# Attention scores from halves of the array's rows instead of the whole array

## The chip, the cores and the metric

The kernel runs on one core of one Trainium2 chip. The metric is the device time of one execution in microseconds (us); the lower the better. The engines are TensorE (PE, with its loads of the stationary operand as PEld), VectorE (DVE), ScalarE (ACT), GpSimd (POOL) and SyncE (SP), which here only issues transfers (DMAs).

## The reference, cut to what matters

Two layers, each with three branches that read the same normalised input. The change lies in branch A, sliding-window attention over 1024 tokens with 16 query heads of 64 channels; 4 query heads share a group of keys and values.

```
s = jnp.einsum('bnqkgd,bnskd->bnkgqs', q, kk).astype(jnp.float32) * (A_HEAD_DIM ** -0.5)
...
s = s - slopes[:, :, None, None] * dist.astype(jnp.float32)
s = jnp.where(valid[None, :, None, None], s, -jnp.inf)
...
m = jnp.maximum(jnp.max(s, axis=-1, keepdims=True), sink)
p = jnp.exp(s - m)
probs = (p / (jnp.sum(p, axis=-1, keepdims=True) + jnp.exp(sink - m))).astype(vv.dtype)
o = jnp.einsum('bnkgqs,bnskd->bnqkgd', probs, vv)
```

Each block of 128 queries sees the 128 keys of its own block and the 128 before it. Branch B is gated linear attention, branch C an S5 scan; a projection in front and one behind hold most of the products.

## The kernel before

Everything is float32. A product that has to be exact is made of float32r products, which PE takes in one pass where a float32 product takes two passes: an operand is split into hi (rounded to float32r, by ACT) and lo (the rest, by DVE), and hi x hi, hi x lo and lo x hi are added up. `split` (L50) does it for weights, inputs and the like. Projections (`proj_T`, L387 to L389) give 24 such products of 128 x 512 for each half of the tokens.

In attention the channels of a head fill only 64 of the array's 128 rows. The kernel uses the other 64 for lo: `proj_aq` evicts a projection of two heads into `qs`, per head hi on partitions 0 to 63 and lo on 64 to 127, with two instructions each on ACT (L473) and DVE (L474), 64 partitions a piece. `keys` writes hi and lo of a group's keys into `kd`, each on both halves of the partitions, with two copies on ACT (L452) and two subtractions on DVE (L453). `attn_block` then needs two products of 128 rows per head (L588, L589): stationary [q hi; q lo], streamed [k hi; k hi] and [k lo; k lo], 256 columns each. So a block of 128 queries and two heads costs four products. Both heads' scores lie in one PSUM room, `sc`, taken from 6 common rooms (a bank each); projections have 2 of their own.

Behind the scores come, for each head, bias and maximum (DVE, L594), exponential (ACT, L599) and division (DVE, L601, L603), four transposes of the probabilities into `pT` (PE, L609), a split into `ph` and `pl` (ACT L52, DVE L53), the products with the values (PE, L619, L620) and the sum of their halves (ACT L622, DVE L626). Blocks overlap: `attention` emits for each of 8 pairs of heads and 8 blocks the first stage of a block, then pieces of the S5 scan (`s5_step`), of modulation sums (L135, L145) and of queued projections (`pump`), then the next stages of the blocks in flight. So 64 blocks a layer, 128 in all, are spread over the two attention stages. `keys` and `values` of the next group are called behind the last block of a group (first half of the tokens) and behind the second block of the next (second half).

A scheduler puts each engine's instructions in order; PE, DVE and ACT then run theirs strictly in that order, and SP its transfers.

Of the kernel before, what the change touches and what calls it, by code (L numbers as in the profile page):

```python
# [24 lines left out]
P = 128  # L25
# [10 lines left out]
# parts of M at the end of a layer: heads of branch A in pairs, branch B, branch C  # L36
# [5 lines left out]
class Trunk:  # L42
# [7 lines left out]
    def split(self, hi, lo, src):  # L50
        """hi = src rounded to float32r, lo = src - hi (exact in float32r)."""
        self.nc.scalar.copy(hi, src)  # L52
        self.nc.vector.tensor_tensor(out=lo, in0=src, in1=hi.bitcast(F32), op=ALU.subtract)  # L53
# [31 lines left out]
    def queue(self, name, gen, units=4):  # L85
        """units of products in a generator whose first step is to load; units = 0: no such step."""
        self.q.append([name, gen, units, units > 0])

    def prefetch(self, n=0):
        """emit the loads of the queue's entry n ahead of its products."""  # L90
        if len(self.q) > n and self.q[n][3]:
            next(self.q[n][1])
            self.q[n][3] = False

    def unit(self):
        """emit one unit of the queue; False if it is empty."""
# [18 lines left out]
    def finish(self, name=None):  # L115
        """emit the queue up to the end of the named entry, or all of it."""
# [7 lines left out]
    def rstd(self, ss, n, w=1):  # L124
        """(ss / n + EPS) ** -0.5 on a small tile, in place."""
# [12 lines left out]
    def mod_part(self, l, j):  # L138
        """512 columns at a time; j: shift 0, 1, scale 2, 3, gate * g_post 4, 5."""
# [42 lines left out]
    # ---- first layer's input: norm, transpose, modulation, split, by blocks of 256 columns; a_v grows with them  # L182
    def startup(self):
# [5 lines left out]
        # c, b_mod and g_pre with D on partitions  # L189
# [12 lines left out]
        def load(n):  # L202
            """256 rows of 512 columns for shift or scale."""
# [12 lines left out]
        # silu(c) = c * (1 + tanh(c / 2)) / 2  # L216
# [6 lines left out]
        # sums that grow side by side in a bank are one group, opened by a product with zeros  # L223
# [22 lines left out]
        # rows of w_mod whose products run on the tensor engine; the others are summed first  # L246
        direct = (((2, 5), (1, 2, 5)), ((2,), (5,)))

        def mods(b):
            """shift and scale of a half of the columns."""  # L250
# [27 lines left out]
        def prep(b, h):  # L278
            """half of the columns, half of the tokens."""
# [78 lines left out]
    def wsplit(self, shape, srcs):  # L358
        """load weights in chunks of 512 to 544 columns a partition and split them."""
# [15 lines left out]
    def proj_T(self, l, c0, sink):  # L375
        """Columns c0..c0+128 of h @ w_in, transposed: [128, tokens] in two halves."""
# [18 lines left out]
    def proj_tok(self, l, cols, sink):  # L395
        """Columns of h @ w_in, tokens on partitions; cols: list of (first, number)."""
# [38 lines left out]
    def proj_av(self, l):  # L435
        """a_v with tokens on partitions."""
# [3 lines left out]
    def proj_ak(self, l, pair):  # L440
        """keys of two groups, kept in float32."""
# [3 lines left out]
    def keys(self, g, half):  # L445
        """keys of a group in two parts, each on both halves of the partitions, half of the tokens."""
        nc = self.nc
        sl = slice(half * 512, (half + 1) * 512)
        src = self.M[64 * (g % 2):64 * (g % 2) + 64, 12 + g // 2, sl]
        for e in range(2):  # L450
            ps_ = slice(64 * e, 64 * e + 64)
            nc.scalar.copy(self.kd[ps_, 0, sl], src)  # L452
            nc.vector.tensor_tensor(out=self.kd[ps_, 1, sl], in0=src, in1=self.kd[ps_, 0, sl].bitcast(F32),  # L453
                                    op=ALU.subtract)

    def values(self, g, half):
        """values of a group in two parts, half of the tokens."""
# [6 lines left out]
    def proj_aq(self, l, pair):  # L464
        """queries of two heads, scaled, in two parts on the two halves of the partitions."""
# [3 lines left out]
        def sink(pj, half, ts_):  # L469
            q = qs[half]  # L470
            for h in range(2):
                src = pj[64 * h:64 * h + 64, :]
                nc.scalar.mul(q[0:64, h, :], src, 0.125)  # L473
                nc.vector.scalar_tensor_tensor(out=q[64:128, h, :], in0=src, scalar=0.125,  # L474
                                               in1=q[0:64, h, :].bitcast(F32),
                                               op0=ALU.mult, op1=ALU.subtract)
        return self.proj_T(l, OFF_AQ + pair * P, sink)

    def advance(self, flight, gen=None):
        """entries in flight: each advances by a stage as a new one enters."""  # L480
# [6 lines left out]
    def attention(self, l, side):  # L487
        """all pairs of heads; the S5 scans, the GLU and projections run between the blocks."""
# [30 lines left out]
        for pair in range(8):  # L519
# [10 lines left out]
            for b in range(NT):  # L530
# [24 lines left out]
                if pr == 1 and b == NT - 1 and g < 3:  # L555
                    self.finish(f"k{(g + 1) // 2}")
                    self.keys(g + 1, 0)
                    self.values(g + 1, 0)
# [3 lines left out]
        while flight:  # L562
# [3 lines left out]
            for _ in range(2):  # L566
                # the last two units gate what the last blocks put out
# [6 lines left out]
    def attn_block(self, pair, b, qs, bias):  # L574
        """128 queries of two heads; softmax over the scores of two blocks of keys and the sink."""
# [8 lines left out]
        sc = self.psum("sc")  # L584
        for h in range(2):
            lhs = qs[:, h, (b % 4) * P:(b % 4 + 1) * P]
            dst = sc[:, h * 256:(h + 1) * 256]
# [1014 lines left out]
```

## Time and profile before

| | |
|---|---|
| time, median of 3 runs | 1860.26 us (1858.48 to 1860.90) |
| span of the profiled execution | 1860.8 us, within the range of the runs |
| PE busy | 1749.4 us, 94% |
| DVE busy | 1353.2 us, 73% |
| ACT busy | 859.7 us, 46% |
| attention stages | about 360 to 780 us and 1240 to 1660 us |

PE's products are pipelined: a row's time runs to the modelled end of the product, which overlaps the next one, so the distance between two starts says what a product costs PE. A projection product of 512 streamed columns starts 0.23 us after the one before it. In the chain of work that ended last each piece is followed back to what released it. A float32 product has two rows for its two passes, a float32r product one.

### The profile page before, as it was taken

How to read it: one execution, taken by the hardware profiler on the slowest of the kernel's cores; microseconds unless marked ns; L12 is line 12 of the kernel's file. 1: busy time of each engine (PE TensorE's matmuls, PEld its weight loads, DVE VectorE, ACT ScalarE, POOL GpSimd, SP SyncE). 2: the span in 40 equal slices, each digit the busy share in tenths (PEclk: the TensorE clock that was granted, in tenths of full speed). 3: DMA queues.
4: the chain of work that ended last, by engine and by line, in shares of the span. 5: the costliest groups of instructions: out<-in, count | busy, mean ns of one | idle time of the engine just before them, and what ended most of it. 6: DMA issues, size and time to landing. Idle time of an engine off the chain costs nothing.

```text
span 1860.8 us, 28251 instructions
## 1 busy us (share of the span) xinstructions
PE 1749.4 (94%) x9403; PEld 1458.5 (78%) x9403; DVE 1353.2 (73%) x2975; ACT 859.7 (46%) x1973; POOL 589.0 (32%) x1005
## 2 busy tenths in 40 slices
PE   7999799999989989999998999999999899999998
PEld 5987688887777677788778878888878767878876
DVE  6986796579999798647676765954898978873534
ACT  5233333445556565446663242423555656642433
POOL 4279750212343454002217850401323511000100
PEclk7999999999999999999998999999999999999999
DMA  8143402235542322335464432222345111113342
GB/s 308 31 108 125 131 29 74 65 113 171 170 142 69 114 74 76 101 125 184 169 199 95 137 102 57 57 60 65 104 128 150 52 46 41 35 51 134 105 165 101
DMA packets 239385, 198.24 MB, mean 107 GB/s; under 512 B 49596, under 2 KB 195068, under 8 KB 239240
## 3 DMA queue, kind: packets, MB, share of 16 engines
q1 hardware_dynamic: 211640, 172.54, 30.9%
q10 hardware_dynamic: 25536, 16.80, 2.9%
q0 software_dynamic: 2064, 7.11, 1.0%
q8 instruction: 74, 1.21, 0.3%
q14 instruction: 71, 0.58, 0.1%
HBM read 163.13 MB, written 37.46 MB: 108 GB/s over the span
## 4 chain that ended last, share of the span: by engine, by line
PE 61%; DVE 21%; ACT 5%; issue 5%; POOL 4%; DMA 4%; SPq 0%; ACTq 0%; DVEq 0%; POOLq 0%
PE py L1472 14%; PE pj L387 9%; PE pj L389 9%; PE pj L388 9%; DVE wlo L53 2%; PE pj L1472 2%; PE pa L884 2%; PE pj L1370 2%; DVE p L594 2%; DVE pl L53 1%; PE pT L609 1%; PE pj L408 1%; PE pj L410 1%; PE pj L409 1%; DVE p L603 1%
## 5 line engine op out<-in xcount | busy, mean ns | idle before, releaser
L387 PE MATMUL pj<-H,whi 128*128 128x512 f32 x1088 | 442.8, 407 | 10.6 <-DVE M L1386 6.4
L389 PE MATMUL pj<-H,wlo 128*128 128x512 f32 x1088 | 431.7, 397 | 5.5 <-DVE wlo L53 5.5
L388 PE MATMUL pj<-H,whi 128*128 128x512 f32 x1088 | 431.0, 396 | 0.0
L53 DVE TENSOR_TENSOR wlo<-wraw,whi 128x512 fp32r<-128x512 f32 (+1 forms) x320 | 238.6, 765 | 87.2 <-ACT whi L52 86.5
L52 ACT CAST whi<-wraw 128x512 fp32r<-128x512 f32 (+1 forms) x320 | 191.4, 618 | 185.3 <-PE pj L388 108.9
L387 PEld LDWEIGHTS pj<-H,whi 128*128 128x128 f32 x1088 | 207.6, 191 | 56.4 <-DVE M L1386 7.2
L389 PEld LDWEIGHTS pj<-H,wlo 128*128 128x128 f32 x1088 | 207.1, 190 | 54.3 <-DVE wlo L53 7.4
L388 PEld LDWEIGHTS pj<-H,whi 128*128 128x128 f32 x1088 | 207.6, 191 | 40.9 <-issue 1.3
L599 ACT ACTIVATE p<-p,st 128x257 f32<-128x257 f32 (+1 forms) x256 | 125.7, 492 | 153.4 <-DVE st L594 133.4
L53 DVE TENSOR_TENSOR mlo<-M,mhi 128x384 fp32r<-128x384 f32 (+2 forms) x80 | 53.4, 675 | 141.8 <-ACT mhi L52 135.7
L1472 PE MATMUL py<-whi,mhi 128*128 128x512 f32 x448 | 142.4, 397 | 6.6 <-ACT whi L52 3.5
L1472 PE MATMUL py<-wlo,mhi 128*128 128x512 f32 x448 | 144.8, 396 | 0.6 <-DVE wlo L53 0.5
L1472 PE MATMUL py<-whi,mlo 128*128 128x512 f32 x448 | 143.3, 394 | 0.7 <-DVE mlo L53 0.7
L1493 POOL TENSOR_SCALAR yrs<-yss 128x1 f32<-128x1 f32 x16 | 6.7, 418 | 376.5 <-ACT junk L1489 375.4
L52 ACT CAST mhi<-M 128x384 fp32r<-128x384 f32 (+2 forms) x80 | 50.3, 634 | 158.4 <-PE pj L1472 92.7
L594 DVE CUSTOM_DVE_ANT_0 p<-sc,bias,sink 128x256 f32<-128x256 f32 (+1 forms) x256 | 111.4, 463 | 9.2 <-PE sc L589 8.1
L583 POOL COPY p<-sink 128x2 f32<-128x2 f32 x128 | 36.0, 283 | 220.9 <-PE pT L609 102.2
L1472 PEld LDWEIGHTS py<-whi,mhi 128*128 128x128 f32 x448 | 83.1, 188 | 28.9 <-ACT whi L52 6.7
L1472 PEld LDWEIGHTS py<-wlo,mhi 128*128 128x128 f32 x448 | 84.2, 188 | 22.9 <-DVE wlo L53 4.1
L1472 PEld LDWEIGHTS py<-whi,mlo 128*128 128x128 f32 x448 | 84.1, 188 | 20.0 <-DVE mlo L53 1.5
L410 PE MATMUL pj<-wlo,H 128*128 128x256 f32 (+1 forms) x320 | 92.9, 292 | 6.3 <-DVE wlo L53 6.3
L408 PE MATMUL pj<-whi,H 128*128 128x256 f32 (+1 forms) x320 | 93.6, 293 | 3.7 <-DVE hv L346 2.7
(380 smaller groups left out, 3931.8 us busy)
## 6 DMA issues: line engine op xcount, KB each, us to landing
wraw<-in_w_in_dram SPq DMA_DIRECT2D x160, 256.0 KB
wraw<-in_w_out_dram SPq DMA_DIRECT2D x160, 256.0 KB
wraw<-in_w_mod_dram SPq DMA_DIRECT2D x64, 256.0 KB
M<-s5tab SPq DMA_DIRECT2D x32, 256.0 KB
M<-s5turn SPq DMA_DIRECT2D x64, 128.0 KB
M<-in_w_mod_dram SPq DMA_DIRECT2D x10, 512.0 KB
s5tab<-O ACTq DMA_DIRECT2D x8, 512.0 KB
s5tab<-G ACTq DMA_DIRECT2D x8, 512.0 KB
```

The costliest lines, as they stand in the source:

```text
L52: self.nc.scalar.copy(hi, src)
L53: self.nc.vector.tensor_tensor(out=lo, in0=src, in1=hi.bitcast(F32), op=ALU.subtract)
L387: nc.tensor.matmul(pj, hi, hh, start=(k == 0), stop=False)
L388: nc.tensor.matmul(pj, hi, hl, start=False, stop=False)
L389: nc.tensor.matmul(pj, lo, hh, start=False, stop=(k == KD - 1))
L408: nc.tensor.matmul(pj[:, :N], hh, hi, start=(k == 0), stop=False)
L410: nc.tensor.matmul(pj[:, :N], hh, lo, start=False, stop=(k == KD - 1))
L594: nc.vector.tensor_tensor_reduce(out=p[:, h, 0:n], in0=sc[:, h * 256:h * 256 + n], in1=bias[:, h, o0:o0 + n], scale=-1.0, scalar=self.sink ...
L599: nc.scalar.activation(p[:, h, 0:n + 1], p[:, h, 0:n + 1], AF.Exp, bias=neg[:, h:h + 1], scale=-1.0, accum_out=den[:, h:h + 1])
L884: nc.tensor.matmul(pa[:, j * P:(j + 1) * P], X[:, c * P:(c + 1) * P], xq[:, :, c * 64:(c + 1) * 64], start=True, stop=True)
L1370: nc.tensor.matmul(pz, wg[:, k, :], self.M[:, MIX_C[k], ts_], start=(k == 0), stop=(k == 3))
L1472: self.nc.tensor.matmul(py[t, h], lhs, ws[h][w][:, 0, :], start=(n == 0 and first), stop=(n == N - 1 and last))
```

## The change

`keys` splits a group's keys once, on the half of the partitions on which they lie, and one DMA per half of the tokens (256 KB, on the SP queue) copies hi and lo to the other half. It is called for the first half of the next group's tokens behind the sixth block of the group's second pair, where it was behind the eighth; `values` stays there. `proj_aq` evicts both heads at once, hi and lo into separate columns, with one instruction of 128 partitions on ACT and one on DVE. `attn_block` makes the scores of a head from three products of 64 rows, hi x hi, hi x lo and lo x hi; head 0 uses partitions and array rows 0 to 63, head 1 the others, in turn. Each head has its own room `sc`, so a block takes two of the six. The product lo x lo, which was in the sum, is left out. Comments are left out of the diff.

```
     def keys(self, g, half):
         nc = self.nc
         sl = slice(half * 512, (half + 1) * 512)
-        src = self.M[64 * (g % 2):64 * (g % 2) + 64, 12 + g // 2, sl]
-        for e in range(2):
-            ps_ = slice(64 * e, 64 * e + 64)
-            nc.scalar.copy(self.kd[ps_, 0, sl], src)
-            nc.vector.tensor_tensor(out=self.kd[ps_, 1, sl], in0=src, in1=self.kd[ps_, 0, sl].bitcast(F32),
-                                    op=ALU.subtract)
+        here, there = (slice(64 * e, 64 * e + 64) for e in (g % 2, 1 - g % 2))
+        src = self.M[here, 12 + g // 2, sl]
+        self.split(self.kd[here, 0, sl], self.kd[here, 1, sl], src)
+        nc.sync.dma_start(self.kd[there, :, sl].bitcast(F32), self.kd[here, :, sl].bitcast(F32))
...
             q = qs[half]
-            for h in range(2):
-                src = pj[64 * h:64 * h + 64, :]
-                nc.scalar.mul(q[0:64, h, :], src, 0.125)
-                nc.vector.scalar_tensor_tensor(out=q[64:128, h, :], in0=src, scalar=0.125,
-                                               in1=q[0:64, h, :].bitcast(F32),
-                                               op0=ALU.mult, op1=ALU.subtract)
+            nc.scalar.mul(q[:, 0, :], pj, 0.125)
+            nc.vector.scalar_tensor_tensor(out=q[:, 1, :], in0=pj, scalar=0.125, in1=q[:, 0, :].bitcast(F32),
+                                           op0=ALU.mult, op1=ALU.subtract)
...
-                if pr == 1 and b == NT - 1 and g < 3:
+                if pr == 1 and b == 5 and g < 3:
                     self.finish(f"k{(g + 1) // 2}")
                     self.keys(g + 1, 0)
+                elif pr == 1 and b == NT - 1 and g < 3:
                     self.values(g + 1, 0)
...
-        sc = self.psum("sc")
-        for h in range(2):
-            lhs = qs[:, h, (b % 4) * P:(b % 4 + 1) * P]
-            dst = sc[:, h * 256:(h + 1) * 256]
-            nc.tensor.matmul(dst, lhs, kd[:, 0, k0:k0 + 256], start=True, stop=False)
-            nc.tensor.matmul(dst, lhs, kd[:, 1, k0:k0 + 256], start=False, stop=True)
+        sc = [self.psum("sc") for _ in range(2)]
+        for x, y in ((0, 0), (0, 1), (1, 0)):
+            for h in range(2):
+                rows = slice(64 * h, 64 * h + 64)
+                nc.tensor.matmul(sc[h][:, 0:256], qs[rows, x, (b % 4) * P:(b % 4 + 1) * P],
+                                 kd[rows, y, k0:k0 + 256], start=(x + y == 0), stop=(x == 1))
...
-            nc.vector.tensor_tensor_reduce(out=p[:, h, 0:n], in0=sc[:, h * 256:h * 256 + n],
+            nc.vector.tensor_tensor_reduce(out=p[:, h, 0:n], in0=sc[h][:, 0:n],
```

What the scheduler makes of it shows at three places (line numbers of the changed kernel are three lower from the query eviction on: L585 is the score product, L606 the transpose, L616 and L617 the products with the values). First PE at a block in the middle of a layer, before:

```order
L609 MATMUL pT_6711<-ident_74,p_6613 128x128 [waits PE_49]
L609 MATMUL pT_6711<-ident_74,p_6613 128x128 x3
L588 MATMUL sc_6722<-kd_3433,qs_5529 128x256
L589 MATMUL sc_6722<-kd_3433,qs_5529 128x256
L588 MATMUL sc_6722<-kd_3433,qs_5529 128x256
L589 MATMUL sc_6722<-kd_3433,qs_5529 128x256
L387 MATMUL pj_6739<-H_72,whi_6524 128x512
L388 MATMUL pj_6739<-H_72,whi_6524 128x512
```

and at such a block (the first of a pair of heads, hence two transposes) of the changed kernel:

```order
L606 MATMUL pT_6750<-ident_74,p_6648 128x128 [waits PE_49]
L606 MATMUL pT_6750<-ident_74,p_6648 128x128
L585 MATMUL sc_6759<-kd_3433,qs_5581 128x256 [waits PE_49]
L585 MATMUL sc_6760<-kd_3433,qs_5581 128x256 [waits PE_49]
L585 MATMUL sc_6759<-kd_3433,qs_5581 128x256
L585 MATMUL sc_6760<-kd_3433,qs_5581 128x256
L585 MATMUL sc_6759<-kd_3433,qs_5581 128x256
L585 MATMUL sc_6760<-kd_3433,qs_5581 128x256
L387 MATMUL pj_6726<-H_72,whi_6268 128x512
L388 MATMUL pj_6726<-H_72,whi_6268 128x512
```

The six products stand together, the heads in turn, and what stands in front of and behind them is as before; so it is at 124 of 128 blocks. Second, PE at one of the other four blocks of the changed kernel, early in the first layer:

```order
L606 MATMUL pT_5663<-ident_74,p_5483 128x128 x3
L585 MATMUL sc_5674<-kd_3433,qs_3611 128x256 [waits DVE_49]
L617 MATMUL po_5652<-pl_5573,vg_3434 128x256 [waits DVE_49]
L616 MATMUL po_5652<-ph_5572,vg_3434 128x256
L617 MATMUL po_5652<-pl_5573,vg_3434 128x256
L585 MATMUL sc_5675<-kd_3433,qs_3611 128x256 [waits Activation_49]
L585 MATMUL sc_5674<-kd_3433,qs_3611 128x256
L585 MATMUL sc_5675<-kd_3433,qs_3611 128x256
L585 MATMUL sc_5674<-kd_3433,qs_3611 128x256
L387 MATMUL pj_5619<-H_72,whi_5608 128x512 [waits Activation_49]
L388 MATMUL pj_5619<-H_72,whi_5608 128x512
L585 MATMUL sc_5675<-kd_3433,qs_3611 128x256
```

Here the score products of the two rooms, sc_5674 and sc_5675, are torn apart by other products, and both first ones wait for an engine that empties a room. Some 50 score products of the changed kernel wait for DVE, where three did before. Third, the SP queue in the second half of the first layer's attention, in the changed kernel:

```order
L145 DMA wraw_6104<-in_w_mod_dram 128x512 [waits DMAHW4_49,DMAHW1_49,DVE_49]
L145 DMA wraw_6178<-in_w_mod_dram 128x512 [waits DMAHW2_49,DVE_49]
L452 DMA kd_3433<-kd_3433 64x2x512 [waits DVE_49,PE_49]
L145 DMA wraw_6232<-in_w_mod_dram 128x512 [waits DMAHW3_49,DVE_49]
L1364 DMA wraw_6252<-in_s5_w_glu_dram 128x4x128 [waits DMAHW4_49,DVE_49]
L370 DMA wraw_6261<-in_w_in_dram 128x4x128 [waits DMAHW5_49,DVE_49]
```

The copy of the keys (L452) waits there for DVE's lo and for PE's last reading of the old keys, and the weight loads (wraw) behind it wait with it; before, the same loads followed one another directly.

## Rows read from the trace of the kernel before

**Rows 1.** The page: busy time with share and instructions, and the chain's shares.

```profile
PE 1749.4 (94%) x9403; PEld 1458.5 (78%) x9403; DVE 1353.2 (73%) x2975; ACT 859.7 (46%) x1973; POOL 589.0 (32%) x1005
PE 61%; DVE 21%; ACT 5%; issue 5%; POOL 4%; DMA 4%; SPq 0%; ACTq 0%; DVEq 0%; POOLq 0%
```

**Rows 2.** Busy time by stage: PE, PEld, DVE, ACT, POOL, clock, DMA.

```profile
360.00:780.00 420.00, 392.63 (x2054) 321.51 (x2055) 363.13 (x965) 227.93 (x584) 139.03 (x223) 0.98 0.37 110
1240.00:1660.00 420.00, 402.58 (x2180) 332.70 (x2179) 335.91 (x925) 236.87 (x645) 102.44 (x192) 0.99 0.26 74
```

**Rows 3.** PE's waits, 386 to 780 us: total us, times, longest.

```profile
PE po L620 <- DVE pl L53: 9.7, 10, 1.7
...
PE po L619 <- ACT ph L52: 3.5, 4, 2.3
...
PE pj L1370 <- DMA wraw<-in_s_w_glu_dram: 0.3, 1, 0.3
```

**Rows 4.** PE's waits, 1301 to 1660 us.

```profile
PE po L620 <- DVE pl L53: 6.1, 8, 1.9
...
PE pj L387 <- DVE M L1377: 0.3, 1, 0.3
```

**Rows 5.** Tiles qs and kd: count, ns min/median/max, first and last start.

```profile
L588 PE MATMUL sc<-kd,qs x256: 276/288/562, 386.0 to 1649.8; 128*128 128x256 f32 x128
...
L473 ACT ACTIVATE qs<-pj x64: 571/594/598, 366.8 to 1597.1; 64x512 fp32r<-64x512 f32 x64
L474 DVE SCALAR_TENSOR_TENSOR qs<-pj,qs x64: 675/690/696, 367.4 to 1599.0; 64x512 fp32r<-64x512 f32 x64
...
  ACT qs L473: 24.4, 22
...
L453 DVE TENSOR_TENSOR kd<-M,kd x32: 671/687/1105, 362.7 to 1591.6; 64x512 fp32r<-64x512 f32 x32
```

**Rows 6.** PE in order of time, one block: start, us, instruction.

```profile
645.42 0.60 PE L609 MATMUL pT<-ident,p 128*128 128x128 f32 x4
...
646.34 0.39 PE L387 MATMUL pj<-H,whi 128*128 128x512 f32 x1
```

**Rows 7.** PE in order of time, transposes of branch B.

```profile
227.18 1.09 PE L800 MATMUL pk<-ident,A 128*128 128x128 f32 x8
228.03 0.48 PE L389 MATMUL pj<-H,wlo 128*128 128x512 f32 x1
228.34 0.40 PE L387 MATMUL pj<-H,whi 128*128 128x512 f32 x1
```

**Rows 8.** PE in order of time, state products on halves of columns.

```profile
1145.83 1.09 PE L811 MATMUL pu<-M,A 128*64 128x128 f32 x16
1146.85 0.50 PE L387 MATMUL pj<-H,whi 128*128 128x512 f32 x1
```

**Rows 9.** PE in order of time, gate products on 16 rows.

```profile
1074.39 0.39 PE L389 MATMUL pj<-H,wlo 128*128 128x512 f32 x1
1074.71 1.98 PE L759 MATMUL pz<-M,wa 16*128 16x512 f32 x4
1076.62 0.50 PE L387 MATMUL pj<-H,whi 128*128 128x512 f32 x1
1076.95 0.39 PE L388 MATMUL pj<-H,whi 128*128 128x512 f32 x1
1077.18 0.40 PE L389 MATMUL pj<-H,wlo 128*128 128x512 f32 x1
```

**Rows 10.** The chain: start, us, piece.

```profile
1510.27 3.45 PE pj L1370 x8
```

**Rows 11.** DVE and ACT in order of time, 128 x 512.

```profile
378.53 0.69 DVE L1386 SCALAR_TENSOR_TENSOR M<-M,pj 128x512 f32<-128x512 f32 x1 [1.50 <-ACT M L1385]
559.46 0.60 ACT L52 CAST whi<-wraw 128x512 fp32r<-128x512 f32 x1
```

**Rows 12.** DMA issues by line: KB each, us to landing.

```profile
s5turn<-cs POOLq DMA_DIRECT2D x8, 256.0 KB, 2.4
```

## Prediction

> **What bounds the kernel now.** I read the page first, for the load of each engine, then busy time by stage, then PE's waits within the two attention stages, and last PE's order of time around single blocks.
>
> PE is busy for 94% of the span and carries 61% of the chain that ended last; DVE carries 21% [rows 1]. Everything that the change edits runs in two stages, 360 to 780 us and 1240 to 1660 us. There PE is busy for 392.6 and 402.6 us of 420 each, DVE for 363 and 336, ACT for 228 and 237 [rows 2]. So PE is the tightest engine and DVE stands close behind it in the first layer. Which of the two ends a given block must be asked block by block. PE's list of waits in the first stage has 12 rows, together 30 waits and 26.5 us, of which three are shown with the first and the last among them [rows 3]; in the second stage it has 5 rows, 21 waits and 13.9 us, of which the first and the last are shown [rows 4]. That is 51 waits and 40 us for 128 blocks (256 rows of the first score product, two a block [rows 5]). So at least 77 blocks run through PE without any wait: there a microsecond more on PE is a microsecond more in the span. In the other blocks PE mostly waits for pl (DVE, L53), ph (ACT, L52) or an operand of the S5 scan (DVE), about 0.8 us a time, and something added to PE in front of such a wait only shortens it.
>
> What a block's scores cost PE now: the four transposes begin at 645.42 and the next projection product at 646.34 [rows 6], 0.92 us. Eight transposes elsewhere take 0.85 us [rows 7], so four take 0.43 and the four score products 0.48 us: 0.12 each, with no gap on either side.
>
> **The change, part by part.** *Six products of 64 rows in place of four of 128.* Two questions decide the price: do the products of two halves run side by side, and what does PE lose when it goes from the whole array to halves and back?
>
> The first has a near relative in the trace. The state products of branch B (L811) are the only ones that go to two halves in turn, though halves of the array's columns. Sixteen of their passes take 1.02 us [rows 8]. Passes of the same 128 streamed columns on the whole array take 0.85/8 = 0.106 us each [rows 7], so sixteen in a row would take 1.70 us. Eight pairs side by side take 0.85, and the 0.17 left is the cost of a change, below. So two halves overlap there completely, loads of the stationary operand included. I take the same for rows: three pairs at 0.12 us, 0.36 us. The other end is no overlap, 6 x 0.12 = 0.72 us.
>
> The second question also has a row. The gate products (L759) use 16 rows of the array, and stand between products of all 128 rows. The product before them starts at 1074.39 and they at 1074.71, 0.32 us instead of the usual 0.23: 0.09 lost. The four take 1.91 us to the start of L387 [rows 9], where eight such passes on the whole array take 3.45 us [rows 10], so four take 1.72: 0.19 lost. The first product after them takes 0.33 instead of 0.23: 0.10 lost. Together 0.38 us for one visit. Some of it is not the rows: L759 is float32 and L387 is float32r, and with the array whole that change alone makes 0.31 of 0.23 [rows 7], 0.08 us. So a visit to another form costs 0.30 to 0.38 us; I take 0.34, since the exit is to a product of 512 columns in most blocks, as in the row. The column case agrees for its inner part: 0.17 within the sixteen passes [rows 8], 0.19 within the four.
>
> The Trainium skill says the same without a price: "TensorEngine Tiling (Array Packing)", Tiling Modes, Key Properties, states that changing the tiling mode drains the engine, and that tiles otherwise work independently. Both halves of that agree with [rows 8, 9].
>
> Sum for a block: 0.36 + 0.34 - 0.48 = +0.22 us of PE time, with +0.18 and +0.26 as the ends for the price of a visit, +0.58 without overlap, and -0.12 if a visit cost nothing. Over 128 blocks +28 us (+23 to +33). In the order, 124 blocks keep their six products together between transposes and the next product; a handful are split by other products and pay two visits, which is under 2 us.
>
> What of it reaches the end: in the 77 blocks without a wait all, 77 x 0.22 = 17 us. In the other 51 blocks 11 us, of which the waits that follow can swallow up to their own length; many are shorter than 0.22 us and some stand behind DVE work that itself started late, so I let a third through, 4 us. Together +21 us. (That is as if 94 blocks paid in full: 77 + 51/3.)
>
> *Queries.* For each half of a projection ACT and DVE now do two instructions of 64 x 512, 0.594 and 0.69 us [rows 5]; 64 of each become 32 of 128 x 512. Instructions of 128 x 512 take 0.60 on ACT and 0.69 on DVE [rows 11], so twice as many partitions cost nothing, and half the instructions go: 32 x 0.69 = 22 us of DVE and 32 x 0.594 = 19 us of ACT. *Keys.* 32 subtractions of 64 x 512, 0.687 us [rows 5], become 16, and so do the copies on ACT, of the size of its query instructions: 11 us of DVE and 10 of ACT. In all DVE loses 33 us and ACT 29 us, about 5% and 6% of their load in the two stages. ACT also stood idle for 24.4 us until DVE had finished one half of a query tile [rows 5], and that ping-pong ends too.
>
> What this relief is worth is bounded by PE's waits, 40 us, and from below by nothing, since off PE's path it costs nothing to be slow. The three rows of waits for pl and ph that are shown come to 19 us [rows 3, 4]. The relief falls in the blocks that evict queries or keys, roughly half of those that wait, so I take 9 us.
>
> *The copy of the keys.* 16 transfers of 256 KB join the SP queue. Nearest in the trace are transfers of 256 KB on POOL's queue, 2.4 us from issue to landing [rows 12]. At the start of the first layer DVE begins to write keys at 362.7 us and the first score product starts at 386.0 [rows 5]. So over 20 us of projections cover the first copy. The move of the first half from the last block to the sixth gives the later ones two to three blocks, over 10 us. A held issue on SP shows only if the copy waits long and a weight load stands behind it that PE needs at once; I count 0, at most 4 us.
>
> *Score rooms.* The scores now take two of the six common PSUM rooms instead of one. In the order some 50 of the score products now wait for DVE, where three did. A room comes back after six requests, which is still more than a block later, and by then its reader has mostly run, since the stages of a block follow one another; so I take 0, with 10 us, a quarter of PE's present waits, as the upper end.
>
> Sum: 1860.8 + 21 - 9 = **1873 us**. The profiled execution's span, 1860.8, lies within the three runs (median 1860.26), so the forecast stands as it is for the median.
>
> **The rivals.**
> *No price for the visit, faster.* If going from whole array to halves of the rows is free, each block gains 0.12 us. Only blocks without a wait feel that, 77 x 0.12 = 9 us, and the relief brings 9: 1842 us. For it: the score products follow transposes, which themselves join onto them without a gap [rows 6]. Against it: [rows 9]. It decides below 0.22 us a visit, where 94 x (0.22 - 0.12) equals the relief. The Trainium skill's tiling page, under Theoretical Speedup, promises up to twofold for a contraction of 64 rows or fewer; that rule taken alone is this case.
> *Even.* A visit at 0.2 to 0.25 us, or a relief of twice my value: 1858 to 1864 us.
> *No overlap.* The two row halves load or stream one after the other: 94 x 0.58 = 55, less 9: 1906 us. Against it stand [rows 8], for it that these are halves of columns with loads of 64 columns, and the new loads have 128.
> *Rooms or queue.* Score products wait for DVE to empty a PSUM room, or weight loads stand behind a key copy: 10 us more, 1883 us. The turn of six rooms speaks against the first, the long cover against the second.
>
> **How the numbers follow.** A measurement of this kernel tells 0.2%, 3.7 us, from no change. Chances: forecast 0.57, no price 0.10, even 0.15, no overlap 0.10, rooms or queue 0.08. Even splits into faster 0.05 and same 0.10. So faster 0.15, same 0.10, slower 0.75. The forecast's own range runs from 1859 (0.18 x 94 = 17, relief 19) to 1894 (0.26 x 128 = 33, no relief); the rooms reach 1900. From 1855 to 1900 leaves out the free visit and the missing overlap, 2 in 10.
>
> **What would show it.** Score products in pairs that start within hundredths of a microsecond, three pairs 0.12 us apart; 0.1 us lost at the entry, as much on the first pair, and 0.1 to 0.2 between the last pair and the second projection product; so 0.7 us from the first score product to L387's start in place of 0.55. DVE's sum 33 us lower, ACT's 29, and PE's waits for pl shorter but not gone. Stages of 360 to 780 and 1240 to 1660 us some 6 us longer each, all others the same. The forecast is wrong if the pairs start 0.12 us apart one by one, if no gap stands at the visits, or if a new wait at the scores names DVE or a DMA with more than 5 us in total.

## The result, and the profile after

The changed kernel takes 1884.30 us (median of 4 runs, 1878.05 to 1894.81) against 1860.58 beside it on the same chip: a ratio of 1.0139, 95% interval 1.0115 to 1.0163. It is slower, by 24 us, where the forecast had 12. On two other chips the same kernel gave 1.0128 [1.0109, 1.0147] and 1.0137 [1.0117, 1.0157].

The page's busy times and shares of the chain, after, beside [rows 1]:

```profile
PE 1777.1 (95%) x9659; PEld 1453.8 (77%) x9659; DVE 1300.2 (69%) x2927; ACT 832.2 (44%) x1925; POOL 591.2 (32%) x1005
PE 67%; DVE 12%; POOL 9%; DMA 5%; issue 3%; ACT 3%; SPq 1%; ACTq 0%; DVEq 0%; POOLq 0%
```

Busy time by stage (columns as in [rows 2]: PE, PEld, DVE, ACT, POOL, clock, DMA):

```profile
360.00:780.00 420.00, 399.94 (x2152) 313.22 (x2153) 341.58 (x931) 209.92 (x553) 135.78 (x222) 0.98 0.38 113
1240.00:1660.00 420.00, 408.71 (x2256) 324.06 (x2255) 305.98 (x866) 217.63 (x602) 101.95 (x191) 1.00 0.28 78
```

DVE and ACT have become lighter and PE heavier, and the chain moved from DVE (21% to 12%) to PE (61% to 67%). The kernel took work off the engine that had time and put it on the one that had almost none.

One block in PE's order of time, after, and the same place in `x1_whole`, the kernel of the first experiment, where the scores are four products of the whole array as before (start, us, instruction):

```profile
650.94 0.60 PE L606 MATMUL pT<-ident,p 128*128 128x128 f32 x4
651.47 0.62 PE L585 MATMUL sc<-kd,qs 64*128 64x256 f32 x6
652.02 0.50 PE L387 MATMUL pj<-H,whi 128*128 128x512 f32 x1
652.35 0.39 PE L388 MATMUL pj<-H,whi 128*128 128x512 f32 x1
```

```profile
639.60 0.60 PE L605 MATMUL pT<-ident,p 128*128 128x128 f32 x4
639.95 0.72 PE L585 MATMUL sc<-kd,qs 128*128 128x256 f32 x4
640.51 0.39 PE L387 MATMUL pj<-H,whi 128*128 128x512 f32 x1
640.74 0.39 PE L388 MATMUL pj<-H,whi 128*128 128x512 f32 x1
```

From the first transpose to L387 it is 1.08 us after and 0.91 with four whole products (0.92 before, [rows 6]). The exit is longer than that: L388 starts 0.33 us behind L387 instead of 0.23. So the block costs PE 0.27 us more, up to L388. The single starts show where: the first score product stands 0.20 us behind the last transpose (0.03 with the whole array, where the second then follows after 0.20 and the others after 0.12); the two halves of a pair start 3 ns apart; pairs follow after 0.22 and 0.115 us; L387 follows the last product after 0.20 (0.12 with the whole array). The forecast's picture was right in kind: pairs run fully side by side, and going to halves and back costs at both ends.

PE's waits in the two attention stages (385 to 800 and 1300 to 1700 us; total us, times, longest), first and last rows of 11 and of 6:

```profile
PE po L617 <- DVE pl L53: 6.7, 6, 2.0
PE po L616 <- ACT ph L52: 5.4, 7, 2.6
PE py L1329 <- DVE s5a L1323: 3.6, 2, 1.9
...
PE sc L585 <- DVE o L623: 1.3, 1, 1.3
...
PE pe L1305 <- DVE st L598: 0.3, 1, 0.3
...
PE po L617 <- DVE pl L53: 4.5, 5, 1.6
...
PE pj L387 <- DVE M L1374: 0.2, 1, 0.2
```

All rows of both lists come to 31.0 us, against 42.3 us for the kernel before in the same stretches. Neither list has a wait for the copy of the keys. There is one wait at a score product, 1.3 us, where the kernel before had two, of 1.1 and 0.5.

How long the score products of a layer take, from the first to the last (tile sc, first and second layer), before, after and in `x1_whole`; before, the last product is one of L589 and starts 0.1 to 0.2 us later:

```profile
L588 PE MATMUL sc<-kd,qs x128: 276/322/562, 386.0 to 755.9; 128*128 128x256 f32 x128
L588 PE MATMUL sc<-kd,qs x128: 276/288/562, 1301.7 to 1649.8; 128*128 128x256 f32 x128
L585 PE MATMUL sc<-kd,qs x384: 270/279/581, 385.6 to 765.1; 64*128 64x256 f32 x192
L585 PE MATMUL sc<-kd,qs x384: 270/279/387, 1312.1 to 1667.1; 64*128 64x256 f32 x192
L585 PE MATMUL sc<-kd,qs x256: 274/282/562, 383.6 to 748.6; 128*128 128x256 f32 x128
L585 PE MATMUL sc<-kd,qs x256: 276/282/562, 1295.3 to 1639.0; 128*128 128x256 f32 x128
```

Both layers together that is 718 us before, 734.5 after (740.9 and 737.6 in two more profiles of the changed kernel) and 708.6 with whole products. So the stages that the change edits are 16 to 23 us longer than before, 20 in the mean, where the forecast looked for some 6 in each.

Tiles qs and kd (count, ns min/median/max, first and last start), beside [rows 5]:

```profile
L469 ACT ACTIVATE qs<-pj x32: 574/596/603, 366.3 to 1609.7; 128x512 fp32r<-128x512 f32 x32
L470 DVE SCALAR_TENSOR_TENSOR qs<-pj,qs x32: 661/682/692, 366.9 to 1610.5; 128x512 fp32r<-128x512 f32 x32
L52 ACT CAST kd<-M x16: 615/618/622, 360.8 to 1595.2; 64x512 fp32r<-64x512 f32 x16
L53 DVE TENSOR_TENSOR kd<-M,kd x16: 669/687/875, 362.3 to 1596.9; 64x512 fp32r<-64x512 f32 x16
```

Half the instructions, each as long as before: 33 us less on DVE, 29 on ACT, as forecast. The page's sum for DVE fell by 53, but `b4_two_rooms` below, whose DVE has the same work as before, shows 1337.8 instead of 1353.2, so some 15 us of that are spread between profiles.

### The profile page after: what moved, and what is told of

It is laid out like the page before. It is cut to its first block, busy times and chain, and to the rows that moved or that the text cites. A ratio compares the mean times of both kernels' runs of the same rounds, so it can differ in the third digit from the quotient of the medians.

```text
span 1876.3 us, 28768 instructions
## 1 busy us (share of the span) xinstructions
PE 1777.1 (95%) x9659; PEld 1453.8 (77%) x9659; DVE 1300.2 (69%) x2927; ACT 832.2 (44%) x1925; POOL 591.2 (32%) x1005
## 4 chain that ended last, share of the span: by engine, by line
PE 67%; DVE 12%; POOL 9%; DMA 5%; issue 3%; ACT 3%; SPq 1%; ACTq 0%; DVEq 0%; POOLq 0%
PE py L1469 14%; PE pj L387 10%; PE pj L389 9%; PE pj L388 9%; PE sc L585 3%; PE pj L1469 2%; PE pT L606 2%; PE pj L1367 2%; PE pa L881 2%; PE po L617 1%; DMA wraw<-in_w_mod_dram 1%; POOL sn L1213 1%; PE po L616 1%; PE pj L408 1%; PE pj L410 1%
## 5 line engine op out<-in xcount | busy, mean ns | idle before, releaser
L387 PE MATMUL pj<-H,whi 128*128 128x512 f32 x1088 | 450.5, 414 | 8.0 <-ACT M L661 5.2
L389 PE MATMUL pj<-H,wlo 128*128 128x512 f32 x1088 | 432.0, 397 | 2.4 <-DVE wlo L53 2.4
L388 PE MATMUL pj<-H,whi 128*128 128x512 f32 x1088 | 431.0, 396 | 0.0
L53 DVE TENSOR_TENSOR wlo<-wraw,whi 128x512 fp32r<-128x512 f32 (+1 forms) x320 | 233.3, 748 | 93.3 <-ACT whi L52 92.3
L387 PEld LDWEIGHTS pj<-H,whi 128*128 128x128 f32 x1088 | 207.6, 191 | 63.2 <-ACT M L661 5.6
L389 PEld LDWEIGHTS pj<-H,wlo 128*128 128x128 f32 x1088 | 206.6, 190 | 50.5 <-DVE wlo L53 3.3
L388 PEld LDWEIGHTS pj<-H,whi 128*128 128x128 f32 x1088 | 208.1, 191 | 41.1 <-issue 1.3
```

The lines of the kernel that those rows point to most:

```text
L387: nc.tensor.matmul(pj, hi, hh, start=(k == 0), stop=False)
L388: nc.tensor.matmul(pj, hi, hl, start=False, stop=False)
L389: nc.tensor.matmul(pj, lo, hh, start=False, stop=(k == KD - 1))
```

## The experiments

Times below are medians; "whole" is the kernel with four whole products. `x1_whole`, its repetition `x11_whole_again`, `x7_one_pair`, `x8_six_whole`, `x10_pair_first`, `x12_three_pairs` and `x13_one_half` compute other scores than the reference, as their expectations say, and are there for their times alone; the others keep the scores. The kernel before stood beside every group of runs; its medians there were 1863 to 1865 us.

**Take the halves away, and serve the halves differently.** `a1_again` is the changed kernel once more. `x1_whole` keeps all of the change but the form of the scores:

```
-        for x, y in ((0, 0), (0, 1), (1, 0)):
-            for h in range(2):
-                rows = slice(64 * h, 64 * h + 64)
-                nc.tensor.matmul(sc[h][:, 0:256], qs[rows, x, ...], kd[rows, y, k0:k0 + 256], ...)
+        for h in range(2):
+            lhs = qs[:, h, (b % 4) * P:(b % 4 + 1) * P]
+            for y in range(2):
+                nc.tensor.matmul(sc[h][:, 0:256], lhs, kd[:, y, k0:k0 + 256], start=(y == 0), stop=(y == 1))
```

> The changed kernel once more, for its spread. Its four runs so far lie between 1878 and 1895 us, with a mean granted clock of 0.979 in the fastest (span 1876.3) and 0.971 in the slowest (span 1893.0); before is at 0.980. If the spread is TensorE's clock (theory C), a mean of 0.008 less over 1890 us is 30 us more at half clock, that is 15 us lost, and every execution's span follows its mean clock: about 1876 + 2 us for each 0.001 below 0.979. If it is something else (waits for PSUM rooms or for the SP queue, theory W), spans differ at equal clocks and the clock explains less than half of the difference.

> Everything of the change kept but the halves: four products of 128 rows a block, as before, into the two rooms (each sums both heads, so the scores are other numbers). Visit theory: PE needs 0.48 us a block as before and no visit, the relief of DVE and ACT stays, so 1845 to 1856 us, faster than before. If the rooms, the key copy or the new order cost the time, it stays above 1865. Clock theory in its strong form (the halves themselves lower the clock): mean clock 0.979 or more in every execution and a spread under 4 us; if the spread stays as wide as that of the changed kernel, the halves are not its cause.

`x2_serial` swaps the two loops, so that head 0's three products are issued before head 1's. `x5_two_blocks` makes the scores of two blocks at once, every second block, in the two halves of the rooms' columns: 64 visits with 12 products each.

> The six products head after head instead of in turn. If the halves overlap only when they alternate, a block needs about 0.24 us more (six starts 0.12 apart instead of three pairs), 128 x 0.24 = 31 us on PE, some 22 us of it in the time: 1895 to 1915 us. If order does not matter, because products of the other half are taken ahead anyway, the same time as the changed kernel.

> Scores of two blocks of queries in one visit: twelve products together, 64 visits instead of 128, same work, the rooms held longer. Visit theory: each visit saved gives back the 0.17 to 0.29 us that entering and leaving cost, 64 x 0.29 = 18 us on PE, 12 to 18 us in the time: 1862 to 1872 us where the changed kernel has 1876 to 1884. If the products themselves (three pairs for two times two) were the cost, no gain. If longer held rooms stall PE, slower than the changed kernel.

Measured: `a1_again` 1886.63 us; `x1_whole` 1851.30, ratio 0.9940 [0.9921, 0.9959]; `x2_serial` 1887.76, ratio 1.0131 [1.0113, 1.0150]; `x5_two_blocks` 1877.77, ratio 1.0074 [1.0053, 1.0096].

The form of the scores alone is worth 35 us, and the rest of the change, taken together, is a gain. The clock theory in its strong form failed: the six runs of `x1_whole` spread over 7.6 us, and one had 0.976. Of the two cases for `x2_serial` the second came true: the order of the two heads' products makes no difference. PE in `x2_serial`:

```profile
654.46 0.60 PE L606 MATMUL pT<-ident,p 128*128 128x128 f32 x4
654.99 0.63 PE L585 MATMUL sc<-kd,qs 64*128 64x256 f32 x6
655.54 0.50 PE L387 MATMUL pj<-H,whi 128*128 128x512 f32 x1
655.88 0.39 PE L388 MATMUL pj<-H,whi 128*128 128x512 f32 x1
```

Three products of one half and then three of the other stand in the program, yet L387 starts 0.55 us behind the first, as in the changed kernel, and the starts in the trace come in pairs 10 ns apart. Products of one half alone start 0.12 us apart (`x13_one_half` below), so each pair must hold one of each half: here PE did not run its products strictly in the program's order, as "The kernel before" has it. In `x5_two_blocks` one visit serves two blocks:

```profile
668.62 0.60 PE L612 MATMUL pT<-ident,p 128*128 128x128 f32 x4
669.14 0.98 PE L588 MATMUL sc<-kd,qs 64*128 64x256 f32 x12
670.05 0.50 PE L387 MATMUL pj<-H,whi 128*128 128x512 f32 x1
670.39 0.39 PE L388 MATMUL pj<-H,whi 128*128 128x512 f32 x1
```

From the first product to L387 it is 0.91 us for six pairs, against 0.55 for three: three pairs more cost 0.36 us, 0.12 each, and only the rest is a visit. The time fell by 9 us and not by the 12 to 18 expected; by the table below the two stages did gain 16, and the rest was lost outside them.

**Price the visit and the added time apart.** `x8_six_whole` has six products of the whole array per block: more PE time, no visit. `x7_one_pair` has four whole products and behind them one pair of 64 rows into columns 256 to 511 of the rooms; `x10_pair_first` has that pair in front of the four.

```
+        for h in range(2):
+            rows = slice(64 * h, 64 * h + 64)
+            nc.tensor.matmul(sc[h][:, 256:512], qs[rows, 1, (b % 4) * P:(b % 4 + 1) * P],
+                             kd[rows, 0, k0:k0 + 256], start=True, stop=True)
```

> Six score products per block as in the changed kernel, but each on all 128 rows (the lo x hi one repeats hi x hi, so the scores are other numbers). PE never leaves the whole array; against the kernel with four such products, 1851.3 us, each block costs PE two products more, 0.24 us, 31 us in all. If all that is added to PE in front of a block's waits lands in the end: 1882 us. If the blocks that wait let only a third through, as the forecast counted (94 of 128 blocks in full): 1874 us. Granted clock: if going to halves lowers it, this kernel keeps the 0.981 of the kernel with four; if a busier PE lowers it, it falls to 0.976 as in the changed kernel.

> Four products of 128 rows per block, then one pair of products of 64 rows into columns of the rooms that nobody reads (the scores are other numbers). This is one visit to halves with one pair in it. If a visit costs 0.39 us and a pair 0.11, each block pays 0.50 us more than the kernel with four whole products (1851.3 us): 1915 us if all of it lands, 1898 us if it lands as 94 blocks of 128. If the visit costs nothing and the pair alone counts: 1862 to 1865 us. If the two halves ran one after the other at no price for the visit, two products of 0.12: 1882 us.

> The kernel with one visit of one pair of 64 rows a block, but the visit in front of the four whole score products instead of behind them (scores are other numbers). The PE time of a visit is the same 0.50 us a block; now the scores, and so DVE's softmax, come 0.5 us later too. If only PE's own path counts: 1899 us, as with the visit behind (of 64 us that PE pays, 45 to 48 us landed). If a delay that lies in front of the scores lets less go through the waits, as the changed kernel's does (28 to 35 of 35 us landed): 1905 to 1913 us.

> The kernel with four whole products on the operands of the changed kernel once more (scores are other numbers), as the reference on this chip: 0.994 of the kernel before, 1851 to 1854 us.

Measured: `x8_six_whole` 1883.35 us, ratio 1.0095 [1.0078, 1.0111]; `x7_one_pair` 1899.45, 1.0190 [1.0174, 1.0206]; `x10_pair_first` 1897.75, 1.0182 [1.0150, 1.0213]; `x11_whole_again` 1852.69, 0.9946 [0.9926, 0.9965]. PE in `x7_one_pair`:

```profile
606.12 0.60 PE L609 MATMUL pT<-ident,p 128*128 128x128 f32 x4
606.48 0.72 PE L585 MATMUL sc<-kd,qs 128*128 128x256 f32 x4
607.13 0.38 PE L588 MATMUL sc<-kd,qs 64*128 64x256 f32 x2
607.44 0.50 PE L387 MATMUL pj<-H,whi 128*128 128x512 f32 x1
607.78 0.39 PE L388 MATMUL pj<-H,whi 128*128 128x512 f32 x1
```

From the first transpose to L388 this is 1.66 us against 1.14: one pair costs 0.51 to 0.52, of which 0.12 is the pair and 0.39 the visit. But PE's 65 us come out as 47, and it isn't the place of the visit: in front of the scores it costs the same as behind, the first of the two cases for `x10_pair_first`. `x8_six_whole`, with 31 us more on PE, is 31 us slower than the whole-array kernels. The waits tell where the rest of the 65 went. PE's second list (1300 to 1700 us) in `x7_one_pair`, whole:

```profile
PE po L619 <- ACT ph L52: 2.1, 1, 2.1
PE po L620 <- DVE pl L53: 1.3, 3, 0.8
```

3.4 us are left there of 14.0, and 16.9 of 23.6 in the first stage: 17 us of waits have been filled.

**Double the visit's content, or forbid the overlap; and the clock.** `x12_three_pairs` is `x7_one_pair` with three pairs in the visit. `x13_one_half` is the changed kernel with all six products on rows 0 to 63:

```
-                rows = slice(64 * h, 64 * h + 64)
+                rows = slice(0, 64)
```

> The changed kernel once more, on the chip of the next two, for its granted clock. If its products in halves lower the clock: 0.975 to 0.976, three thousandths below the kernel before on the same chip, and a ratio of 1.013. If the low clock of the two samples so far was chance: within 0.001 of the kernel before, and a ratio of 1.010 to 1.011, since a thousandth of the clock is worth 1.2 us over all runs so far.

> Four whole score products a block, and behind them one visit with three pairs of 64 rows into columns that nobody reads, where there was one pair (scores are other numbers). Two pairs more are 0.23 us a block, 29 us; PE's waits had only 20 us left with one pair, so nearly all of it lands: 1898 + 25 to 29 = 1923 to 1928 us. Clock: 0.975 if paired products lower it, 0.978 as with one pair if they don't.

> The changed kernel with both heads' six products on rows 0 to 63 (head 1 gets head 0's operands, so its scores are other numbers): the same visits, but no two products can run side by side. Six at 0.12 us and a visit at 0.39 instead of four whole ones, 0.48: 0.63 us a block, 81 us, of which PE's waits swallow up to 20: 1853 + 61 = 1914 us, at most 1934. If the two halves bring nothing even in the changed kernel, the same time as that, 1885 us. Clock: 0.975 if going to halves lowers it, 0.978 or more if two products at once do.

Measured: `a3_again` 1887.23 us, 1.0137; `x12_three_pairs` 1932.64, 1.0369 [1.0348, 1.0390]; `x13_one_half` 1910.24, 1.0254 [1.0233, 1.0276]. PE in `x13_one_half`:

```profile
608.24 0.60 PE L606 MATMUL pT<-ident,p 128*128 128x128 f32 x4
608.77 0.97 PE L585 MATMUL sc<-kd,qs 64*128 64x256 f32 x6
609.67 0.50 PE L387 MATMUL pj<-H,whi 128*128 128x512 f32 x1
610.01 0.39 PE L388 MATMUL pj<-H,whi 128*128 128x512 f32 x1
```

Without two halves at work the six take 0.90 us to L387 instead of 0.55: the overlap in the changed kernel is real and complete. This is the forecast's rival of no overlap, made to happen; it priced that at 1906 us. `x12_three_pairs` came out 5 us above the top of its expectation, and `x13_one_half` 4 below its own. `a3_again` had a clock of 0.975 against 0.979 for the kernel before on the same chip, as expected if the products in halves lower it; but `x12_three_pairs` and `x13_one_half`, halves too, had 0.980 and 0.979.

All of these against the whole-array kernels (1852 us, two sets of runs). The first column is the time from the last transpose to L388, less 0.818 us, which is what it is with whole products; it is the median over the 65 to 69 blocks whose scores stand there in one piece between a transpose and L387. For `x5_two_blocks` it is half of what a visit with two blocks' scores costs more than two blocks with whole products. Waits filled are what the sum of both lists is below 38.0 us, that of the whole-array kernels (two profiles); with two blocks a visit the sum is above it, 42.9. The account is the second column less the third. Stages are the stretches from the first to the last score product of both layers in the profiled execution, less 709.0 us, the mean of the two whole-array profiles. Measured is the whole time over 1852 us. The clock is the mean granted clock over the runs, 0.981 for the whole-array kernels (in the traces each stretch is granted in full, 2.4 GHz, or by half, 1.2 GHz).

| kernel | PE, us a block | x 128 | waits filled | account | stages | measured | clock |
|---|---|---|---|---|---|---|---|
| six whole | 0.239 | 30.6 | 1.1 | 29 | 29 | 31 | 0.979 |
| changed (3 sets) | 0.272 | 34.8 | 6.9 | 28 | 29 | 34 | 0.975 |
| one pair behind | 0.507 | 64.9 | 17.7 | 47 | 45 | 47 | 0.978 |
| one pair first | 0.512 | 65.5 | 17.3 | 48 | 46 | 46 | 0.980 |
| one half only | 0.627 | 80.3 | 20.5 | 60 | 59 | 58 | 0.979 |
| three pairs behind | 0.748 | 95.7 | 16.3 | 79 | 78 | 81 | 0.980 |
| two blocks a visit | 0.076 | 9.7 | -4.9 | 15 | 13 | 26 | 0.973 |

PE's added time, less the waits that it fills, is the lengthening of the two attention stages within 3 us for all seven kernels: the price of a visit holds there without any other term. The whole time agrees within some 2 us for five. The two that stand out are the changed kernel, by 6 us, and the two blocks a visit, by 11. Their surplus lies outside the stages or in the spread of executions: in its profiled execution `x5_two_blocks` is 12 us longer than the whole-array kernels outside them; the changed kernel is 2 us longer there in its three profiles, whose spans in all differ from those of the whole-array kernels by 30 us, where the medians differ by 34.

Both also have the lowest clock. Over 179 runs of all kernels, taken against each kernel's own mean, a clock 0.001 lower goes with a time 1.15 us longer (a fitted line, with a correlation of -0.79; theory C of `a1_again` had 2 us); six thousandths below 0.981 are 7 us, eight are 9. That is the size of both gaps, but the same term would move the other five by 1 to 4 us, three of them away from the measurement, so it isn't shown that the clock makes them. Why the clock is lower there isn't settled either. `x12_three_pairs` has as many pairs and visits as the changed kernel and keeps 0.980, `x13_one_half` has the visits alone and keeps 0.979, so neither pairs nor visits by themselves lower it. Those two compute other scores, though, and whether the values take part was not tested.

**The rest of the change, piece by piece.** `b1_keys_once` is the kernel before with the new `keys` and its earlier call. `b4_two_rooms` is the kernel before with a room for each head. `b2_all_whole` adds to `b1_keys_once` queries that are split over whole partitions, with lo brought to the other half by DMAs, so that the four products of 128 rows can stay:

```
...
+            nc.scalar.mul(q[:, 0, :], pj, 0.125)
+            nc.scalar.mul(q[64:128, 1, :], pj[64:128, :], 0.125)
+            nc.vector.scalar_tensor_tensor(out=lo, in0=pj, scalar=0.125, in1=q[:, 0, :].bitcast(F32),
+                                           op0=ALU.mult, op1=ALU.subtract)
+            nc.sync.dma_start(q[0:64, 1, :].bitcast(F32), lo[64:128, :].bitcast(F32))
+            nc.sync.dma_start(q[64:128, 0, :].bitcast(F32), lo[0:64, :].bitcast(F32))
```

`b3_whole_rooms` is `b2_all_whole` with the two rooms.

> The kernel before, with the changed kernel's keys only: split once, copied by a DMA, and called for the next group behind the sixth block. Queries and score products as before. If the relief of DVE and ACT is worth what it was in the kernel with four whole products (9 to 14 us for all 33 us of DVE) in proportion, a third of it: 1856 to 1858 us. If it is the earlier call alone that helps: 1850 us. If the relief lies in the queries alone or the copy's wait on the queue eats it: 1860 us or above.

> The kernel before, with its four products of 128 rows, and the relief of the change: keys once with a copy, queries split once over whole partitions by one DVE instruction, ACT's hi by one whole and one half instruction, and lo brought to the other half by two DMAs of 128 KB for each half of a projection (64 in all). If the relief is what made the kernel with four whole products faster: 1850 to 1853 us. If the DMAs on SP hold weight loads, or the wait for the copied lo shows at the first block of each half: 1860 us or more.

> The kernel before with one edit: each head's scores in a PSUM room of its own. If the forecast was right that the rooms cost and bring nothing: 1860 to 1863 us, a ratio of 0.998 to 1.002. If the rooms are part of the gain of 9 to 14 us that the kernel with four whole products showed: 1856 us. If they make score products wait: 1866 us or more.

> The kernel before with keys once and copied, queries split over whole partitions with lo brought over by DMA, and two rooms for the scores: all of the change except that the scores stay four products of 128 rows. If the rooms make up the difference between 0.9975 (the same without them) and 0.994 (four whole products without DMAs of queries): 0.994, 1852 us. If the difference is the price of the 64 DMAs: 0.9975, 1858 us.

Measured: `b1_keys_once` 1860.87 us, ratio 0.9988 [0.9973, 1.0002]; `b4_two_rooms` 1863.99, 0.9995 [0.9979, 1.0011]; `b2_all_whole` 1858.38, 0.9975 [0.9960, 0.9990]; `b3_whole_rooms` 1855.54, 0.9955 [0.9933, 0.9976], where before had 1863.50 beside it. Keys and rooms, each alone, bring nothing that can be told from no change. `x1_whole`, which adds the queries to both, lies below `b1_keys_once` by more than the intervals; whether the queries alone do that, or the queries and the rooms together, stays open, since the intervals of `b2_all_whole` and `b3_whole_rooms` overlap. `b2_all_whole` and `b3_whole_rooms` both lie between the two cases of their expectations, so the price of the 64 DMAs stays open too. `b3_whole_rooms` beats both kernels, by 8 us and by some 30: it keeps the relief and the results, and leaves out the halves. Its page and its query rows:

```profile
PE 1740.3 (94%) x9403; PEld 1453.5 (79%) x9403; DVE 1307.2 (71%) x2927; ACT 852.9 (46%) x1957; POOL 594.7 (32%) x1005
L470 ACT ACTIVATE qs<-pj x32: 572/598/605, 365.0 to 1585.0; 128x512 fp32r<-128x512 f32 x32
L471 ACT ACTIVATE qs<-pj x32: 592/593/597, 365.6 to 1585.7; 64x512 fp32r<-64x512 f32 x32
L472 DVE SCALAR_TENSOR_TENSOR lo<-pj,qs x32: 653/691/693, 366.2 to 1586.3; 128x512 fp32r<-128x512 f32 x32
```

DVE has the changed kernel's load, and PE the 9403 products of the kernel before.

## Why the forecast had the direction and half the size

*The visit: right in kind, too cheap. This is the step that failed.* The forecast had 0.30 to 0.38 us and took 0.34, because by [rows 7] it put 0.08 us of the gate products' 0.38 [rows 9] down to their being float32 beside float32r. That deduction was a misreading. The last transpose of [rows 7] stands alone here:

```profile
228.00 0.27 PE L800 MATMUL pk<-ident,A 128*128 128x128 f32 x1
```

The transposes follow one another after 0.11 us, but L389 starts 0.03 us behind this one, and the 0.31 to the next product only make up for that: from the last transpose to L387 it is 0.34 us, which is one transpose (0.11) and one product (0.23). Nothing is lost there, and nothing was to be deducted. The runs agree: in `x12_three_pairs` the visit stands between float32r products on both sides and still costs 0.40 us (0.748 less three pairs of 0.117), 0.39 in `x7_one_pair`. The undiminished row had it, 0.38, and in the same four pieces as here, about 0.1 us each: at the entry, behind the first product or pair in the new form, at the exit, and behind the first product after it. So a block costs 0.27 us of PE time, not 0.22, and 128 blocks 35 us, not 28: the term was 7 us too small. The sign of 0.7 us from the first score product to L387 did not show (0.55), because the loss at the entry lies in front of that product and the last one behind L387.

The Trainium skill ("TensorEngine Tiling (Array Packing)", Tiling Modes, Key Properties) states that a change of mode drains the engine. The trace agrees at the entry of `x7_one_pair`, where the pair starts 0.21 us behind the last whole product and not 0.12; but that is a quarter of the price. The first product behind each change is followed late as well: 0.22 us from the first pair to the second in `x12_three_pairs`, and 0.34 from L387 to L388.

*What of it reaches the end: right in size, in part by luck.* The forecast let 7 of 28 us vanish in PE's waits; in three profiles of the changed kernel 6.9 of 35 us vanished. Its reason, a fixed share of the blocks, doesn't hold: `x8_six_whole` filled 1 us with 31, `x7_one_pair` 18 with 65.

*The overlap: right.* Pairs start 3 ns apart at 0.115 to 0.12 us a pair; `x13_one_half` shows what it would be without.

*The relief: right in size, 9 us forecast.* With whole products the same operands bring medians 11 and 14 us below before in two sets of runs (means: 11 and 12, and 7 and 9 when brought to one clock by the fitted line). `b3_whole_rooms` brings 8. In the traces the two stages are 7 to 10 us shorter than before in all three. Where it comes from is shown only in part: PE's lists of waits are 4.3 us shorter with whole products (42.3 to 38.0), and 3.0 in `b3_whole_rooms` (39.3). The keys, a third of DVE's relief, show nothing that can be told from no change when they stand alone; a third of 8 us would lie within that interval.

*Copy of the keys and rooms: right, nothing.* Ratios of 0.9988 and 0.9995 when each is alone, and no wait for either of more than 1.3 us.

*The granted clock: not in the sum.* The kernel before has a mean of 0.9785 in its 70 runs with a listed clock, the changed one 0.975 in 13. By the fitted line that would be 4 us. It is a correlation with the time, not an experiment on the clock.

Together: 35 of PE time, less 7 for waits, less 8 for the relief: 20 us. That is what the two stages are longer than before in the traces of the changed kernel, 16 to 23, 20 in the mean. Measured in the whole time: 23.7, 21.6 and 23.6. The last 2 to 4 us stay open; the clock's 4 would cover them, but that isn't shown. One reading helped to hide all this: the changed kernel's profiled execution had a clock of 0.979 and the shortest of all its times, 1878.05 us, so its trace shows a span only 15.5 us longer than that of before (1876.3 and 1860.8). That is 3 us from the 12 of the forecast, and 8 below the medians. Spans are also 1.8 us below the time of their execution, so the forecast of 1873 was made from a number that belongs to a time of about 1862.6.

## What to carry to other kernels

Two halves of the array's rows do twice the work of one in the same time, but a visit from whole-array products to halves and back cost PE 0.39 us here, a little more than three whole products of 256 columns; even two blocks' scores in a visit, six pairs, didn't pay for it. By the same numbers (0.39 us a visit, and 0.12 saved by three pairs in place of four whole products) it would take four blocks' scores; that is an estimate, and no run tried it. Take a neighbour's measured price whole until the single starts show what to deduct: a long interval behind a product that started early is no loss. When an edit joins a gain on a slack engine with a loss on the tight one, run the two apart: here the slack engine's part alone was the better kernel.

## What the runs showed that was not expected

- The order in which products for the two halves stand in the program didn't matter: three and three gave the same pairs (10 ns apart instead of 3) and the same time, 1887.76 against 1886.63 us.
- Added PE time doesn't fill waits in proportion: 31 us filled 1 us of 38, 65 us filled 18, and 96 us only 16.
- The kernel's mean granted clock differs between versions by up to 0.008 (0.973 to 0.981) with PE busy for 94% to 95% in all of them; by the fitted line that goes with 9 us, but what lowers it, and whether it makes the time, stays open.
